# Layer 1's state-space base tables made during layer 0's experts, in the place of the turned tokens, and the second rotation table folded away

## The chip, the cores and the metric

One core of a Trainium2 chip runs the whole kernel in one launch. The metric is device time in microseconds (us), the median of several executions; a profile of one further execution shows where the time goes. The engines are TensorE (PE in the rows, PEld is its weight load), VectorE (DVE), ScalarE (ACT), GpSimd (POOL) and SyncE (SP), which issues most of the DMA transfers. Everything is fp32.

## The reference, cut to what matters

Two layers work on 256 latent and 256 context tokens of width 1024. In each, one projection feeds three mixers, of which the first is a bidirectional diagonal state-space layer (S5); then come an output projection, norms, and a mixture of 64 experts (top 8 a token) with a shared expert.

```python
step = jnp.exp(log_step)[..., None]
a_bar = jnp.exp(lam * step)                      # lam complex, 16 groups x 64 states, 2 directions
b_bar = ((a_bar - 1.0) / lam)[..., None] * b_mat
bu = jnp.einsum('blgc,gpc->blgp', ug, b_bar)
# s_t = a_bar * s_(t-1) + bu_t, forward and backward, context first, then latent
y = einsum(st_f, c_mat[0]).real + einsum(st_b, c_mat[1]).real + ug * d_skip
...
scores = sigmoid(h @ router_w)                   # group-limited top 8, then the experts
out = sum over chosen experts of gate * (silu(h @ w_gate) * (h @ w_up)) @ w_down  + shared
```

The tables that the state-space layer needs depend on parameters alone, not on tokens.

## The kernel before, in words

The program is written as Python generators, woven into one another; a scheduler then orders the instructions on each engine, and waits are semaphores. So an engine executes strictly in an order that is fixed when the program is built, and the text of the code tells that order only roughly.

Layer 0 goes: mixer (0 to about 322 us), `post` (output projection, norms, router; about 322 to 392), experts (about 450 to 1083), combination of the experts' outputs (1083 to 1146). Layer 1 follows with the same stages on the latent tokens alone behind its mixer.

The state-space layer works on chunks of 8 tokens. `s5_prep` (line 474) makes the tables, in this order: exponentials, sine and cosine of 128x16 tiles (`exact_exp`, line 455); `PW`, the powers 0 to 8 of a; `bb`, b_bar; `PA`, powers of a, in the other direction reversed; then `products(q, MT)` for each quarter q of the 16 groups: KT on VectorE (three operations of 128x512 for each of two parts), MT on GpSimd (likewise three), m (TensorE turns MT, ScalarE copies it to M1), kk (KT times bb), kp (kk plus the skip term) and the store of kp to `kd` in DRAM, from where `T` is loaded back. Between the quarters `rotations()` makes `dec`, `Rin` (powers of a's turn per chunk, 64 of them, by doubling), `Rout` (the same times a), and at its end turns half of Rin around by eight copies. Both layers do all of this within their own mixer.

`s5_main` (line 698) then runs four quarters: bu (TensorE) -> rA, rB, Y (VectorE, times Rin) -> scan E with `dec` -> rA, rB, Z (times Rout) -> s5y (TensorE). Projections (`uvs`, `gos`, `rest` in `mixer`, line 1210) run between: pT is a projection with the channels on the partitions (512 or 256 tokens wide), pN one with the tokens on the partitions (256, 80 or 336 columns); `us`, `va`, `krn`, `gpad` and `og` are copies of their results, and gates, zb, e, Bc, AM, qn and kn are of the other two mixers. qr is the first product behind the state-space part.

`moe` (line 1919) has `fT`, the turned tokens of the layer, 128x8x512 floats in a pool tile, read by the router and the shared expert; `spare` is the buffer of the mixers' outputs (`cat2`), free behind the output projection. Into `spare` and a sixth of `sw` the rows x1 are loaded back for the sum in `merging` (line 1849); `ring` holds the experts' weights, loaded by SP in order as buffers come free. Behind layer 0 the experts' outputs Y are loaded into fT for the combination.

Of the kernel before, what the change touches and what calls it, by code (L numbers as in the profile page):

```python
# [190 lines left out]

def zipper(*gens):
# [57 lines left out]
class Trunk:  # L250
    def __init__(self, ctx, tc, d, dbg=None):
# [25 lines left out]
        self.zeros = self.cp.tile([128, 256], F32, name="zeros")  # L277
# [32 lines left out]
    def clear_y(self, l):  # L310
        for i in range(TOK[l] // 128 + 1):
            self.nc.sync.dma_start(self.Y[l][i * 128:(i + 1) * 128].rearrange("p (r f) -> p r f", r=4),
                                   self.zeros[:, None, :].to_broadcast([128, 4, 256]))
# [160 lines left out]
    def s5_prep(self, l, sp, tp):  # L474

        nc, d, v = self.nc, self.d, self.nc.vector
        pv = tp.tile([128, 48], F32, name="pv")
        turn = []
        pm = tp.tile([128, 1024], F32, name="pm")
        dg = tp.tile([128, 4], F32, name="dg")  # L480
        nc.sync.dma_start(pv, d["s5v"][l])
        yield
        nc.sync.dma_start(pm, d["s5m"][l])
        nc.sync.dma_start(dg, d["s5d"][l])
# [8 lines left out]
        self.exact_exp(er, xr, tp, S, "e2")  # L493
# [15 lines left out]
        PW = tp.tile([128, 2, 16, 9], F32, name="PW")  # L509
# [4 lines left out]
        A = tp.tile([128, 2, 16, 32], F32, name="cmA")  # L514
        B = tp.tile([128, 2, 16, 32], F32, name="cmB")
# [8 lines left out]
        for w in (1, 2, 4):  # L524
            cmul(PW[:, 0, :, w + 1:2 * w + 1], PW[:, 1, :, w + 1:2 * w + 1], PW[:, :, :, 1:w + 1],
                 PW[:, 0, :, w], PW[:, 1, :, w], w)

# [16 lines left out]
        bp = tp.tile([128, 2, 16, 32], F32, name="bb")  # L544
        nc.gpsimd.memset(bp[:, :, :, 16:32], 0.0)
        bb = bp[:, :, :, 0:16]
        bx = pm[:, 0:512].rearrange("p (m g c) -> p m g c", m=2, g=16)
        cmul(bb[:, 0], bb[:, 1], bx, wre, wim, 16)
        cx = pm[:, 512:1024].rearrange("p (m g c) -> p m g c", m=2, g=16)

        PA = tp.tile([128, 2, 16, 8], F32, name="PA")
# [31 lines left out]

        dec = sp.tile([128, 16, 65], F32, name="dec")
        R = sp.tile([128, 2, 16, 64], F32, name="Rin")
        Ra = sp.tile([128, 2, 16, 64], F32, name="Rout")
        nc.gpsimd.memset(dec[:, :, 0], 0.0)
        nc.gpsimd.memset(R[:, 0, :, 0], 1.0)
        nc.gpsimd.memset(R[:, 1, :, 0], 0.0)
        nc.gpsimd.memset(Ra[:, :, :, 0], 0.0)  # L590

        def rotations():

            r8, i8, d8, tA, tB = t("r8"), t("i8"), t("d8"), t("tA"), t("tB")
            cr, ci = cs, sn
            for _ in range(3):
                tt(tA, cr, cr, OP.mult)
                tt(tB, ci, ci, OP.mult)
                v.scalar_tensor_tensor(out=i8, in0=cr, scalar=2.0, in1=ci, op0=OP.mult, op1=OP.mult)
                tt(r8, tA, tB, OP.subtract)  # L600
                cr, ci = r8, i8
            tt(d8, er, er, OP.mult)
            tt(d8, d8, d8, OP.mult)
            tt(d8, d8, d8, OP.mult)
            v.tensor_copy(dec[:, :, 1:65], d8[:, :, None].to_broadcast([128, 16, 64]))
            v.tensor_copy(R[:, 0, :, 1], r8)
            v.tensor_copy(R[:, 1, :, 1], i8)
            X, Y = (z[:, 0].rearrange("p g n -> p (g n)").rearrange("p (m g n) -> p m g n", m=2, g=16) for z in (A, B))

            def turn(o, o0, a0, n, yre, yim):  # L610

                x, sh = R[:, :, :, a0:a0 + n], [128, 2, 16, n]
                tt(X[:, :, :, :n], x, yre[:, None, :, None].to_broadcast(sh), OP.mult)
                tt(Y[:, :, :, :n], x, yim[:, None, :, None].to_broadcast(sh), OP.mult)
                tt(o[:, 0, :, o0:o0 + n], X[:, 0, :, :n], Y[:, 1, :, :n], OP.subtract)
                tt(o[:, 1, :, o0:o0 + n], X[:, 1, :, :n], Y[:, 0, :, :n], OP.add)

            for w in (1, 2, 4, 8):
                turn(R, w + 1, 1, w, R[:, 0, :, w], R[:, 1, :, w])
            yield  # L620
            for o, a, n in ((17, 1, 16), (33, 1, 16), (49, 17, 15)):
                w = 16 if o == 17 else 32
                turn(R, o, a, n, R[:, 0, :, w], R[:, 1, :, w])
            yield
            for a, n in ((0, 16), (16, 16)):
                turn(Ra, a + 1, a, n, are, aim)
            yield
            for a, n in ((32, 16), (48, 15)):
                turn(Ra, a + 1, a, n, are, aim)

# [45 lines left out]
        for _ in turns:  # L676
            pass
# [1355 lines left out]
```

## Time and profile before

| | |
|---|---|
| time, 3 runs | 1990.81 us median (1990.21 to 1991.92) |
| profiled execution | 1989.93 us, of which its span 1988.1 |
| granted TensorE clock, mean | 0.956 |
| TensorE busy | 1802.0 us, 91% |
| VectorE, GpSimd, ScalarE busy | 813.2, 456.1, 379.5 us |

The span is what the trace covers; 1.8 us of the execution lie around it. Busy shares are means over stages that have different limits. In the timelines a row is a group of like instructions that follow one another: its start, its length, engine, line, operation, what it writes and reads, and in brackets how long the engine stood before it and what ended that.

### The profile page before, as it was taken

The numbers are of one execution on the slowest core, as the hardware profiler recorded it, in microseconds if no ns is written. First come the engines' busy times: TensorE is split into PE (matmuls) and PEld (weight loads), VectorE is DVE, ScalarE is ACT, GpSimd is POOL, SyncE is SP. The second block draws the span as 40 slices with busy tenths as digits, with TensorE's granted clock in tenths as the row PEclk, the third lists the DMA queues.
The fourth block names the chain that finished last, engine by engine and source line by source line (L and its number), as shares of the span: only waits on it lengthen the run. The fifth ranks groups of instructions, "written<-read, shape, count | busy, mean of one in ns | idle before, by whom it ended". The sixth has DMA issues, their size and how long they took to land. (4 is left out here: it accounts for less than half of the span.)

```text
span 1988.1 us, 29110 instructions
## 1 busy us (share of the span) xinstructions
PE 1802.0 (91%) x10161; PEld 851.0 (43%) x10161; DVE 813.2 (41%) x2298; ACT 379.5 (19%) x739; POOL 456.1 (23%) x453
## 2 busy tenths in 40 slices
PE   6998999879999999899997178899899999999992
PEld 2554665523334333233332055665543354433340
DVE  6856664731223432222121598764731222312113
ACT  2245331201111111001111313341301011110000
POOL 3120211232223232332221551002101211111223
PEclk7999999989999999999999588999999999999996
DMA  8442567399999999999997423256499999899672
GB/s 321 140 96 101 178 250 293 116 319 358 298 326 340 360 323 293 386 377 339 344 297 232 163 75 64 75 213 258 182 372 343 398 353 358 304 385 355 234 261 69
DMA packets 153922, 524.16 MB, mean 264 GB/s; under 512 B 28787, under 2 KB 37939, under 8 KB 145068
## 3 DMA queue, kind: packets, MB, share of 16 engines
q1 hardware_dynamic: 135228, 480.36, 65.1%
q0 software_dynamic: 18544, 41.90, 9.5%
q8 instruction: 82, 1.34, 0.3%
q14 instruction: 68, 0.56, 0.1%
HBM read 531.12 MB, written 47.61 MB: 291 GB/s over the span
## 5 line engine op out<-in xcount | busy, mean ns | idle before, releaser
L1785 PE MATMUL gu<-ring,xT 128*32 128x512 f32 (+5 forms) x2896 | 645.7, 602 | 18.2 <-DMA ring<-in_exp_w 17.7
L1785 PEld LDWEIGHTS gu<-ring,xT 128*32 128x32 f32 (+5 forms) x2896 | 193.7, 129 | 399.3 <-issue 321.2
L1798 PE MATMUL dn<-ring,hT 128*32 128x512 f32 (+5 forms) x1448 | 330.0, 597 | 4.8 <-DMA ring<-in_exp_w 4.0
L1808 POOL DMA_INDIRECT Y<-xo,gi x79 | 119.9, 1518 | 610.8 <-DMA Y<-xo,gi 140.5
L1681 DVE TENSOR_TENSOR hh<-gu,sg 128x256 f32<-128x256 f32 (+4 forms) x86 | 36.5, 424 | 523.2 <-ACT sg L1680 503.7
L1798 PEld LDWEIGHTS dn<-ring,hT 128*32 128x32 f32 (+5 forms) x1448 | 103.1, 128 | 183.2 <-issue 155.7
L1808 POOL DMA_INDIRECT Y<-xo,si x66 | 91.0, 1379 | 302.6 <-DMA Y<-xo,gi 217.4
L1803 DVE TENSOR_SCALAR xo<-dn,gc 128x512 f32<-128x512 f32 (+5 forms) x80 | 60.0, 751 | 229.0 <-PE dn L1798 215.6
L1680 ACT ACTIVATE sg<-gu 128x256 f32<-128x256 f32 (+4 forms) x86 | 32.8, 384 | 586.6 <-PE gu L1785 586.3
L443 PE MATMUL pT<-hT,w 128*128 128x512 f32 (+1 forms) x288 | 120.4, 572 | 4.3 <-DMA w<-in_w_mm 2.7
L1760 PEld LDWEIGHTS <-fb 128*128 128x128 bf16 x1536 | 86.3, 99 | 41.9 <-issue 41.9
L1802 ACT ACTIVATE xo<-dn,gc 128x512 f32<-128x512 f32 (+5 forms) x80 | 55.0, 687 | 253.3 <-PE dn L1798 239.2
L1760 PE MATMUL xT<-oneh,fb 128*128 128x128 bf16 (+4 forms) x1536 | 94.6, 220 | 0.0
L1392 PE MATMUL yo<-w,cat 128*128 128x512 f32 x192 | 83.4, 594 | 0.8 <-DMA w<-in_w_out 0.8
L1762 DVE COPY xT<-xT 128x512 f32<-128x512 f32 (+5 forms) x80 | 53.2, 670 | 70.0 <-PE xT L1760 37.2
L1762 ACT COPY xT<-xT 128x512 f32<-128x512 f32 (+5 forms) x80 | 45.8, 573 | 185.4 <-PE xT L1760 135.3
L443 PEld LDWEIGHTS pT<-hT,w 128*128 128x128 f32 x288 | 56.0, 200 | 58.0 <-issue 47.5
L290 PE MATMUL hT<-cst,xt 128*128 128x128 f32 x64 | 14.6, 404 | 59.3 <-ACT xt L1982 55.2
L451 PE MATMUL pN<-w,hT 128*128 128x256 f32 (+2 forms) x256 | 65.0, 414 | 3.0 <-DVE va L1268 3.0
L342 PE MATMUL ada<-w,sil 128*32 128x512 f32 x384 | 57.9, 649 | 10.4 <-DMA w<-in_ada_w 10.4
L1742 POOL DMA_INDIRECT xg<-fd,gi x48 | 50.3, 1047 | 48.2 <-PE xT L290 19.0
L451 PEld LDWEIGHTS pN<-w,hT 128*128 128x128 f32 x256 | 49.2, 203 | 19.9 <-issue 5.2
(546 smaller groups left out, 2071.1 us busy)
## 6 DMA issues: line engine op xcount, KB each, us to landing
ring<-in_exp_w SPq DMA_DIRECT2D x768, 512.0 KB
w<-in_ada_w SPq DMA_DIRECT2D x48, 1024.0 KB
w<-in_w_out SPq DMA_DIRECT2D x8, 1024.0 KB
sw<-in_sh_w SPq DMA_DIRECT2D x2, 3072.0 KB
w<-in_w_uv SPq DMA_DIRECT2D x4, 1024.0 KB
Y<-zeros SPq DMA_DIRECT2D x8, 512.0 KB
w<-in_w_mm SPq DMA_DIRECT2D x4, 1024.0 KB
w<-in_w_qk SPq DMA_DIRECT2D x4, 768.0 KB
```

The costliest lines, as they stand in the source:

```text
L342: nc.tensor.matmul(ps[32 * q:32 * q + 32, :], self.sil[:, k, :], t[:, q * 512:(q + 1) * 512], start=k == 0, stop=k == 7, tile_position=(0, ...
L443: self.nc.tensor.matmul(ps[base:base + m, n0:NT], w[k][:, col:col + m], hT[:, k, n0:NT], start=k == 0, stop=k == 7)
L451: self.nc.tensor.matmul(ps[:, :n], hT[:, k, i * 128:(i + 1) * 128], w[k][:, col:col + n], start=k == 0, stop=k == 7)
L1392: nc.tensor.matmul(st[at][n], cb[:, i * 128:(i + 1) * 128], wo[n][b], start=b == 0, stop=b == 7)
L1742: nc.gpsimd.indirect_dma_start(out=x[col:col + cap], out_offset=None, in_=self.fd, in_offset=bass.IndirectOffsetOnAxis(ap=si[0:cap], axis= ...
L1760: nc.tensor.matmul(o, self.fb[i][:, z, cs], t["oh"][:, i, 0:m], start=at == 0, stop=at + 1 == len(parts))
L1762: (nc.scalar.copy if hh else v.tensor_copy)(o, a)
L1785: nc.tensor.matmul(t["gu"][r, :], t["xt"][:, 2 * c + b, r], ws[j][:, b * 512:(b + 1) * 512], start=c == 0 and b == 0, stop=c == 3 and b == ...
L1798: nc.tensor.matmul(po[n][r, :], t["ht"][:, b, r], ws[b * nr + j][:, n * 512:(n + 1) * 512], start=b == 0, stop=b == 1, **kw)
L1802: nc.scalar.activation(xo[0:m, 0:512], po[0][0:m], AF.Identity, scale=t["gc"][0:m])
L1803: v.tensor_scalar(out=xo[0:m, 512:1024], in0=po[1][0:m], scalar1=t["gc"][0:m], scalar2=None, op0=OP.mult)
L1808: nc.gpsimd.indirect_dma_start(out=self.Y[l], out_offset=bass.IndirectOffsetOnAxis(ap=si[0:cap], axis=0), in_=xo[col:col + cap], in_offset ...
```

## The change

`s5_prep` is split. `s5_base` makes everything up to PA, the new PB (powers 8 to 1), d8 and the rotation table R, 65 wide with a zero ahead; `s5_tables` makes KT, MT, the copies from R, and T. For layer 1 `s5_base` runs as a generator beside layer 0's route and experts: its temporaries are cut out of `spare` (`Carve`), its results lie in a permanent tile `pz` of 16 KB a partition. `pz` is also what fT now is; so the results may be written only when fT's readers are through. Rout falls away: `Ra` is R shifted by one column, and the factor a that it lacks goes into MT, which takes PB in place of the reversed PA. The eight turning copies and the copy to dec leave VectorE; ScalarE's copies in `finish` take their place. The first x1 row block is still loaded ahead of the experts, two more are now loaded among them, and layer 0's Y are loaded into `spare`. The rest keeps the size of memory (the zeros tile half as wide, the overflow loop, which reloads its tokens).

```diff
+        self.pz = self.cp.tile([128, 4096], F32, name="pz")
...
-    def s5_prep(self, l, sp, tp):
+    def s5_base(self, l, tp):
...
+        z = self.s5_views()
+        R, bp, PA, PB, PW, d8 = (z[n] for n in ("R", "bp", "PA", "PB", "PW", "d8"))
...
+        v.tensor_copy(PB[0:64], PW[0:64, :, :, 8:0:-1])
+        v.tensor_copy(PB[64:128], PW[64:128, :, :, 1:9])
...
+        for w in (1, 2, 4, 8):
+            turn(w + 1, 1, w, w)
+        yield
+        for o, a, n in ((17, 1, 16), (33, 1, 16), (49, 17, 15)):
+            turn(o, a, n, 16 if o == 17 else 32)
+            yield
+
+    def s5_tables(self, l, sp, tp, turns):
...
+        def finish():
+
+            nc.gpsimd.memset(dec[:, :, 0], 0.0)
+            nc.scalar.copy(dec[:, :, 1:65], d8[:, :, None].to_broadcast([128, 16, 64]))
+            for m in range(2):
+                nc.scalar.copy(Rin[0:64, m], R[0:64, m, :, 1:65])
+                for h in range(2):
+                    nc.scalar.copy(Rin[64:128, m, :, 32 * h:32 * h + 32], R[64:128, m, :, 1 + 32 * h:33 + 32 * h][:, :, ::-1])
...
-            for a, n in ((0, 16), (16, 16)):
-                turn(Ra, a + 1, a, n, are, aim)
-            yield
-            for a, n in ((32, 16), (48, 15)):
-                turn(Ra, a + 1, a, n, are, aim)
-
-            for m in range(2):
-                for h in range(2):
-                    z = X[64:128].rearrange("p m g n -> p (m g n)").rearrange("p (g n) -> p g n", g=16)
-                    r = R[64:128, m, :, 32 * h:32 * h + 32]
-                    v.tensor_copy(z, r)
-                    v.tensor_copy(r, z[:, :, ::-1])
...
-            rr, ri = (PA[:, m, g, ::-1][:, :, :, None].to_broadcast(sh) for m in range(2))
+            rr, ri = (PB[:, m, g, :, None].to_broadcast(sh) for m in range(2))
...
-        self.tb = dict(KT=KT, M1=M1, T=T, dec=dec, R=R, Ra=Ra)
+        self.tb = dict(KT=KT, M1=M1, T=T, dec=dec, R=Rin, Ra=R[:, :, :, 0:64])
...
     def merging(self, l, acc, sw, spare, tiles):
...
-        if len(tiles) > 3:
-            nc.sync.dma_start(sw[:, 4], self.x1[l][tiles[3] * 128:(tiles[3] + 1) * 128])
+        for i, t in enumerate(tiles):
+            nc.sync.dma_start(spare[:, i * D:(i + 1) * D] if i < 3 else sw[:, 4], self.x1[l][t * 128:(t + 1) * 128])
...
-            merge = self.merging(l, acc, sw, spare, tiles)
-            for i, t in enumerate(tiles[:3]):
-                nc.sync.dma_start(spare[:, i * D:(i + 1) * D], self.x1[l][t * 128:(t + 1) * 128])
+            early = iter(())
+            if not last:
+                early = self.turns = self.s5_base(l + 1, Carve(spare))
+            merge = chain(early, self.merging(l, acc, sw, spare, tiles))
...
-            beside(work, sh, 1 if last else 2)
+            beside(work, chain(sh, early), 1 if last else 2)
...
-            bufs = [fT[:, 2 * i:2 * i + 2].rearrange("p k n -> p (k n)") for i in range(nt)]
+            bufs = [spare[:, i * D:(i + 1) * D] if i < 3 else sw[:, 4] for i in range(nt)]
```

The order on TensorE at the start of layer 1's mixer, behind the two 512-wide pT, before the change (m_8472 and m_8478 are the two halves of quarter 0, m_8548 and m_8554 of quarter 1; 8 of pN is one token tile):

```order
L451 MATMUL pN<-w,hT 128x256 x32
L451 MATMUL pN<-w,hT 128x80 x8
L290 MATMUL m_8472<-cst,MT 128x128 x4
L290 MATMUL m_8478<-cst,MT 128x128 x4
L571 MATMUL kk<-KT_8361,bb 32x128 x8
L571 MATMUL kk<-KT_8362,bb 32x128 x8
L451 MATMUL pN<-w,hT 128x80 x8
L290 MATMUL m_8548<-cst,MT 128x128 x4
L290 MATMUL m_8554<-cst,MT 128x128 x4
```

And the same place after it (m_8445, m_8451 are quarter 0, m_8518, m_8524 quarter 1):

```order
L474 MATMUL pN<-w,hT 128x256 x16
L313 MATMUL m_8445<-cst,MT 128x128 x4
L313 MATMUL m_8451<-cst,MT 128x128 x4
L649 MATMUL kk<-KT_8373,pz 32x128 x8
L649 MATMUL kk<-KT_8374,pz 32x128 x8
L474 MATMUL pN<-w,hT 128x256 x16
L313 MATMUL m_8518<-cst,MT 128x128 x4
L313 MATMUL m_8524<-cst,MT 128x128 x4
L649 MATMUL kk<-KT_8373,pz 32x128 x8
L649 MATMUL kk<-KT_8374,pz 32x128 x8
L474 MATMUL pN<-w,hT 128x80 x8
```

The first quarter's m and kk have moved between the 256-wide projections, and the 80-wide projection that stood ahead of them has gone behind the second quarter. The other two quarters, an 80-wide pN, bu and the two 336-wide pN with a bu between them follow after the change; before it a 336-wide pN stood ahead of quarter 2 and another behind quarter 3, ahead of the first bu.

The order on VectorE ahead of the first state (rA<-bu) of layer 1, before:

```order
L635 COPY cmA<-Rin 64x512
L636 COPY Rin<-cmA 64x16x32
L578 SCALAR_TENSOR_TENSOR dgt<-cst,dg,kk 128x16
L487 TENSOR_TENSOR kp<-kp,dgt 128x16
L578 SCALAR_TENSOR_TENSOR dgt<-cst,dg,kk 128x16
L487 TENSOR_TENSOR kp<-kp,dgt 128x16
L961 TENSOR_SCALAR zb<-za,cols 128x512
L964 SCALAR_TENSOR_TENSOR zb<-za,cols,zb 128x512 x2
L983 SCALAR_TENSOR_TENSOR e_8959<-G 64x512
L701 TENSOR_TENSOR rA<-bu,Rin 128x512
```

After, from the last operation of KT on:

```order
L690 SCALAR_TENSOR_TENSOR KT_8374<-cmA,cmB 128x512
L1305 COPY va<-pN 128x4x64
L656 SCALAR_TENSOR_TENSOR dgt<-cst,dg,kk 128x16
L629 TENSOR_TENSOR kp<-kp,dgt 128x16
L1305 COPY va<-pN 128x4x64 x2
L656 SCALAR_TENSOR_TENSOR dgt<-cst,dg,kk 128x16
L629 TENSOR_TENSOR kp<-kp,dgt 128x16
L1315 COPY gpad<-pN 128x4x4 x2
L656 SCALAR_TENSOR_TENSOR dgt<-cst,dg,kk 128x16
L629 TENSOR_TENSOR kp<-kp,dgt 128x16
```

Two more rows, dgt and kp again, then `gpad<-pN 128x4x4 x2` (the two 336-wide pN) stand behind these, and then rA. Rotations and turning copies are gone, zb and e are behind rA, and all four gpad copies are ahead of it.

The order on VectorE in the fourth state, from its scan E to its Z, after the change:

```order
L761 SCALAR_TENSOR_TENSOR E<-dec,Y 128x260 x2
L1007 TENSOR_TENSOR AM<-G,Bc 64x512
L735 TENSOR_TENSOR rA<-E,pz 128x512
L735 TENSOR_TENSOR rB<-E,pz 128x512
L1028 SCALAR_TENSOR_TENSOR AM<-zero,AM 32x512
L1030 SCALAR_TENSOR_TENSOR AM<-zero,AM 32x256
L1007 TENSOR_TENSOR de<-AM,cst 32x32
L1031 SCALAR_TENSOR_TENSOR AM<-zero,AM 32x256
L1007 TENSOR_TENSOR e_8968<-Bc,AM 64x512
L1007 TENSOR_TENSOR de<-AM,cst 32x32
L1042 TENSOR_SCALAR e_8968<-e_8968 64x512
L735 TENSOR_TENSOR Z<-rA,rB 64x256
```

Before, at that place:

```order
L727 SCALAR_TENSOR_TENSOR E<-dec,Y 128x260 x2
L961 TENSOR_SCALAR zb<-za,cols 128x256
L701 TENSOR_TENSOR rA<-E,Rout 128x512
L701 TENSOR_TENSOR rB<-E,Rout 128x512
L964 SCALAR_TENSOR_TENSOR zb<-za,cols,zb 128x256
L701 TENSOR_TENSOR Z<-rA,rB 64x256
```

Seven operations of the gates (AM, de, e), of which some stood in the earlier states and some behind the last Z, now stand between rB and Z of the last state; zb of the last block has gone behind Z.

## Rows read from the trace of the kernel before

**Rows 1.** Windows: length, busy us (instructions) of PE, PEld, DVE, ACT, POOL; PEclk, DMA, GB/s

```profile
1146.00:1290.00 144.00, 118.77 (x655) 81.76 (x655) 122.16 (x296) 39.09 (x75) 34.52 (x43) 0.89 0.27 74
1290.00:1432.00 142.00, 134.09 (x745) 77.16 (x744) 84.55 (x253) 48.76 (x99) 18.33 (x26) 0.99 0.54 204
1432.00:1950.00 518.00, 513.20 (x3618) 220.08 (x3616) 124.65 (x415) 56.03 (x102) 92.18 (x65) 1.00 0.90 332
```

**Rows 2.** Timeline of TensorE in layer 1's mixer

```profile
1146.43 15.29 PE L443 MATMUL pT<-hT,w 128*128 128x512 f32 x32
1161.56 15.72 PE L451 MATMUL pN<-w,hT 128*128 128x256 f32 x80
...
1181.78 2.35 PE L451 MATMUL pN<-w,hT 128*128 128x80 f32 x16 [3.03 <-DVE va L1268]
1190.73 1.09 PE L290 MATMUL m<-cst,MT 128*128 128x128 f32 x4 [6.60 <-DVE va L1268]
...
1196.55 6.66 PE L451 MATMUL pN<-w,hT 128*128 128x336 f32 x16
...
1216.92 1.89 PE L712 MATMUL bu<-U,M 128*128 128x64 f32 x16
...
1258.52 0.69 PE L746 MATMUL s5y<-KT,Z 128*64 128x128 f32 x2 [5.16 <-DVE Z L701]
...
1270.61 0.45 PE L746 MATMUL s5y<-KT,Z 128*64 128x128 f32 x4 [0.22 <-DVE Z L701]
...
1286.56 0.70 PE L845 MATMUL qr<-qn,w 128*128 128x256 f32 x2 [1.47 <-DVE qn L797]
```

**Rows 3.** Timeline of VectorE in layer 1's mixer

```profile
1148.65 0.17 DVE L460 TENSOR_SCALAR e1xc<-pv 128x16 f32<-128x16 f32 x1
...
1210.23 0.69 DVE L487 TENSOR_TENSOR cmA<-Rin,PW 128x512 f32<-128x512 f32 x1
...
1218.63 0.42 DVE L635 COPY cmA<-Rin 64x512 f32<-64x512 f32 x1
...
1229.46 0.69 DVE L701 TENSOR_TENSOR rA<-bu,Rin 128x512 f32<-128x512 f32 x1
...
1268.83 1.73 DVE L701 TENSOR_TENSOR Z<-rA,rB 64x256 f32<-64x256 f32 x4
```

**Rows 4.** Groups by form, VectorE, 1162 to 1183: busy, mean ns, idle before

```profile
L487 DVE TENSOR_TENSOR cmB<-PA,pm 128x512 f32<-128x512 f32 x4 | 6.4, 1591 | 0.0
L487 DVE TENSOR_TENSOR cmA<-PA,pm 128x512 f32<-128x512 f32 x4 | 4.4, 1104 | 0.0
```

**Rows 5.** The same groups of VectorE from 1206 to 1210, GpSimd idle

```profile
L487 DVE TENSOR_TENSOR cmB<-PA,pm 128x512 f32<-128x512 f32 x2 | 1.4, 684 | 0.0
```

**Rows 6.** Timeline of GpSimd in layer 1's mixer

```profile
1161.40 1.05 POOL L659 TENSOR_TENSOR cmA<-PA,bb 128x512 f32<-128x512 f32 x1 [13.94 <-DVE PA L553]
...
1187.60 1.05 POOL L659 TENSOR_TENSOR cmA<-PA,bb 128x512 f32<-128x512 f32 x1
...
1195.85 1.38 POOL L659 TENSOR_TENSOR MT<-cmA,cmB 128x512 f32<-128x512 f32 x1 [6.14 <-PE m L290]
```

**Rows 7.** Timeline of ScalarE, the end of the combination

```profile
1143.39 1.23 ACT L1982 ACTIVATE xt<-acc,nb,a3rs 128x1024 f32<-128x1024 f32 x1
```

**Rows 8.** Timeline of SP, DMA issues in layer 1's mixer

```profile
1173.84 2.08 SPq L329 DMA_DIRECT2D w<-in_w_mm  x2
1201.65 6.28 SPq L582 DMA_DIRECT2D kd<-kp  x8
```

**Rows 9.** Windows, shorter ones of layer 1's mixer

```profile
1176.00:1180.00 4.00, 2.75 (x52) 2.31 (x51) 3.97 (x5) 1.71 (x5) 3.84 (x4) 1.00 1.00 399
...
1190.00:1205.00 15.00, 11.66 (x100) 7.85 (x101) 14.79 (x28) 3.11 (x8) 5.54 (x4) 0.65 0.02 6
```

**Rows 10.** Timeline of VectorE in layer 0, `post` and experts

```profile
349.41 0.69 DVE L1401 TENSOR_TENSOR pt<-yo,g 128x512 f32<-128x512 f32 x1 [1.93 <-PE yo L1392]
...
495.38 0.42 DVE L1681 TENSOR_TENSOR hh<-gu,sg 128x256 f32<-128x256 f32 x1 [15.56 <-ACT sg L1680]
```

More of the change, by code (lines that the diff above doesn't have):

```diff
@@ L189, in beside, with chain, __init__, tile @@
             next(side, None)
+def chain(*gens):
+    for g in gens:
+        yield from g
+class Carve:
+    def __init__(self, at):
+        self.at, self.n, self.got = at, 0, {}
+    def tile(self, shape, dt, name):
+        if name not in self.got:
+            n = math.prod(shape[1:])
+            self.got[name] = self.at[:, self.n:self.n + n]
+            self.n += n
+            assert self.n <= self.at.shape[1]
+        a = self.got[name]
+        if len(shape) == 4:
+            a = a.rearrange("p (a b c) -> p a b c", a=shape[1], b=shape[2])
+        return a if dt == F32 else a.bitcast(dt)
 def zipper(*gens):
@@ L552, in s5_prep @@
         v.tensor_copy(PA[0:64], PW[0:64, :, :, 0:8])
         v.tensor_copy(PA[64:128], PW[64:128, :, :, 7::-1])
-        yield
+        v.tensor_copy(PB[0:64], PW[0:64, :, :, 8:0:-1])
+        v.tensor_copy(PB[64:128], PW[64:128, :, :, 1:9])
+        r8, i8, tA, tB = t("r8"), t("i8"), t("tA"), t("tB")
+        cr, ci = cs, sn
+        for _ in range(3):
+            tt(tA, cr, cr, OP.mult)
+            tt(tB, ci, ci, OP.mult)
+            v.scalar_tensor_tensor(out=i8, in0=cr, scalar=2.0, in1=ci, op0=OP.mult, op1=OP.mult)
+            tt(r8, tA, tB, OP.subtract)
+            cr, ci = r8, i8
@@ new lines, in s5_base @@
+        for w in (1, 2, 4, 8):
+            turn(w + 1, 1, w, w)
+        yield
+        for o, a, n in ((17, 1, 16), (33, 1, 16), (49, 17, 15)):
+            turn(o, a, n, 16 if o == 17 else 32)
+            yield
+    def s5_tables(self, l, sp, tp, turns):
+        nc, d, v = self.nc, self.d, self.nc.vector
+        z = self.s5_views()
+        R, bp, PA, PB, d8 = (z[n] for n in ("R", "bp", "PA", "PB", "d8"))
+        bb = bp[:, :, :, 0:16]
+        pm = tp.tile([128, 512], F32, name="pmc")
+        dg = tp.tile([128, 4], F32, name="dg")
+        nc.sync.dma_start(pm, d["s5m"][l][:, 512:1024])
+        nc.sync.dma_start(dg, d["s5d"][l])
+        cx = pm.rearrange("p (m g c) -> p m g c", m=2, g=16)
+        tt = lambda o, a, b, op: v.tensor_tensor(out=o, in0=a, in1=b, op=op)
+        A, B = (tp.tile([128, 2, 16, 32], F32, name=n) for n in ("cmA", "cmB")) if l else self.cm
+        turn = []
@@ L640, in s5_prep @@
+        Rin = sp.tile([128, 2, 16, 64], F32, name="Rin")
         for _ in range(pace("turn0", l, 0)):
@@ L677, in s5_prep @@
             pass
+        finish()
         yield
@@ L1224, in mixer @@
         tp = P(ps_, "s5tmp", side="right")
-        prep = self.s5_prep(l, sp, tp)
+        if l == 0:
+            base = self.s5_base(0, tp)
         if l == 0:
@@ L1230, in mixer @@
             next(ada)
-            next(prep)
+            next(base)
             xt = [self.ln_load(l, i) for i in range(4)]
@@ L1238, in mixer @@
             weave(ada)
-            next(prep)
+            for _ in range(4):
+                next(base)
             load("uv")
@@ L1249, in mixer @@
             self.zp = P(zs, "z")
+            self.turns = base
         zp = self.zp
@@ L1309, in states @@
         def states():
-            yield from prep
+            yield from self.s5_tables(l, sp, tp, self.turns)
             ps_.close()
@@ L1923, in moe @@
         units = plan(l)
-        acc = mq.tile([128, nt, D], F32, name="acc")
+        acc = self.pz[:, 2048:].rearrange("p (i n) -> p i n", i=nt) if last else mq.tile([128, nt, D], F32, name="acc")
         with ExitStack() as es:
```

102 lines of the change are left out of this document (44 added, 58 removed).

## The prediction

> **What bounds the kernel now.** I read the profile in the order from stage to instruction. The windows [rows 1] first: the expert stages keep TensorE busy throughout, but between 1146 and 1290, in layer 1's mixer, it works 118.8 of 144 us while VectorE works 122.2. So there VectorE, not TensorE, is the full engine, and this is the stage that the change touches most. The timeline of TensorE [rows 2] tells which wait ends last. After two projections (pT, pN) it stands until VectorE has copied `va` (3.03 and 6.60 us), and its last large wait (5.16) and a small one behind it (0.22) are for Z, the last product of VectorE's state chain. The timeline of VectorE [rows 3] shows why everything is late. From 1148.65 it makes the base of the tables (exponentials, powers, `bb`), and GpSimd, which makes MT, has nothing to do until 1161.40: it waited 13.94 us for PA [rows 6]. Then VectorE works through KT, the rotations (Rin, Rout), the turning copies, and only at 1229.46 begins the first state (rA), though its `bu` was ready at 1218.8 [rows 2]. Idle time of TensorE is 25.2 us in this stage [rows 1], and that is nearly all that there is to win here. To it comes the low clock: granted 0.65 from 1190 to 1205 [rows 9], behind the wait of 6.60. A 336-wide pN takes 6.66 us there, and by its columns it would take 4.8 at the pace of the pN from 1161.56 on (15.72 us for 1104 columns) [rows 2].
>
> **The change part by part.**
>
> *What leaves layer 1's mixer.* The base, 1148.65 to 1161.40, 12.8 us of VectorE. The rotation table R, made among the KT pieces: I take its three wide turns and the four short ones at about the size of Rout's four, which ran from 1210.23 to 1218.63, 8.4 us [rows 3]. Rout itself, 8.4 us. The eight turning copies, 0.42 each, 3.4 us. Some 33 us of VectorE go; TensorE's order cannot give all of it back, so I walk through the new order with the old durations.
>
> *GpSimd.* Its first MT product waits only for the temporaries' place, which the last xt of the combine holds until 1143.39 + 1.23 = 1144.6 [rows 7]. Six pieces took 1161.40 to 1187.60, 4.4 us each; alone I take 3.4 (the cmA of 1187.60, which ran alone, took 1.05, and MT costs a fifth more) [rows 6]. MT has two buffers: the wait of 6.14 at 1195.85 was for TensorE's m of the quarter two before [rows 6]. That wait stays, and shapes what follows: the third quarter's first MT must wait for m of the first.
>
> *VectorE.* KT starts where the base started, 1148.65. Beside GpSimd its operations took 1.10 and 1.59 us, alone 0.68 [rows 4, 5]; I take 1.30, for 24 of them 31.2, with three copies of 0.4 between: KT ends at 1181. The va copy that frees the bank of the second m stands behind the last KT.
>
> *TensorE.* Anchor: pT begins at 1146.43 as before, since the combine ahead of it is the same chain. Two pT end at 1161.56. The 15.72 us of the next row are 4 x 256 + 80 columns, so a 256-wide pN costs 3.65 and an 80-wide 1.1. Two pN: 1168.9. m and kk of a quarter fill 1177.1 to 1178.75 (where the idle 3.03 begins), 1.6: 1170.5. Two pN: 1177.8. m of quarter 1 waits for va at 1181: with kk 1182.3. pN80 1183.4, m and kk of quarter 2 1185. GpSimd's seventh MT was held until m of quarter 1 (1181.7), ends 1183.1, its eighth piece alone 3.4 later, 1186.5: m and kk of quarter 3 end at 1187.8. pN80 1188.9, bu 1190.8 (1216.92 + 1.89 before), pN336 1195.6, bu 1197.4, pN336 1202.2 (at 4.8, since TensorE has now stood little). VectorE has the `gpad` copies of both wide pN in its queue ahead of rA, so rA begins about 1202.5, not when bu is ready at 1190.8. Before it was 1229.46: 27 us earlier.
>
> *The state chain.* It ran from 1229.46 to 1270.56, 41.1 us [rows 3]. In the order after it holds the same four states, the same gate work between them, and now also the AM scans and the zb of the first block; those that went ahead before (zb, e) and those that came after (the end of AM, about 2 us) make no big difference: 41 again, Z ends 1243.6. TensorE will have done its pT by 1232 and stands some 12 us.
>
> *Behind Z.* From 1270.56 to qr at 1286.56 it took 16.0 us [rows 2]. In the new order two 256-wide pT more stand there (half of a 512-wide one, 15.29/4 = 3.8 at most, say 3.6 each), while the gap of 1.47 before qr may close: 22.2. So qr comes at 1265.8, 20.8 us earlier. From there the order of TensorE is the old one and the rest moves along. One deduction: a stand of 12 us is longer than the 6.60 behind which the clock was 0.65; for the first pT after it I take 1.5 us (6.66 against 4.8 is 1.9) [rows 2, 9]. Layer 1: -19.3.
>
> *What is paid in layer 0.* The same base work, 12.8 + 8.4 or some 21 us of VectorE, and two table loads of ScalarE, now lie in the post stage and among the experts. Its long tail (bb, the doubling of R) falls behind the last shared gate product, where VectorE stood 15.56 us [rows 10]; hidden, and if it were not, hh of an expert would be late by up to 8.4. Its head stands in the gap of 1.93 us in which VectorE waited for yo [rows 10], but its first operation waits for a load of `pv` into cat2, which may go out only when TensorE has read that part of cat2 for yo. If the load lands 2 us after, the norm of the third token tile is late by 2 to 4 us; four gaps behind it can take it up. Bounds 0 and 4, I take 1. Two 512 KB loads of x1 move from before the experts into their last third: at 399 GB/s [rows 9] 2.6 us if nothing hides them, 0 if the ring is ahead; I take 0.5. ScalarE's new copies (dec, Rin) and layer 0's own base: modc behind one more product of 0.68, 0.6. In layer 0's mixer Rout and the copies go too, 12 us of VectorE. I count nothing for it: TensorE there works through its projections, and the end of the state chain is fed by bu products whose place in its order stays. Sum +2.
>
> *Sum.* -19.3 + 2 = -17.3. The profiled execution took 1989.93 us, 1.8 more than its span, and the median is 1990.81; from the median this gives 1973.5.
>
> **A rule that speaks against it.** KT and MT ran side by side, and both slowed: 1.59 for 0.68, 4.4 for about 3.4 [rows 4 to 6]. In the new order they run together from the first operation. The Trainium skill ("SBUF — State Buffer", section "SBUF: two separate sides") says that VectorE with two SBUF inputs and GpSimd exclude each other for a whole instruction. By that rule each KT operation beside GpSimd would cost its own 0.68 and one of GpSimd's, 1.05 to 1.3, about 1.8. The trace agrees in part only: 1.3 is the mean, and in 4.4 us of GpSimd's piece fit more than three of VectorE's operations.
>
> **The rivals.**
> 1. *The bigger gain.* VectorE has 20 us less to do, so KT may see less of GpSimd (0.68 instead of 1.30 for the last third saves 5 us), rA comes at 1197 and the clock does not fall: 25 to 29 us at most, the whole idle time of the stage and the slow pN. 1962 to 1968.
> 2. *SP's queue.* The w_mm loads were issued at 1173.84 [rows 8]; in the new order they stand behind the eight kd stores of quarters 0 and 1. kp of these waits behind KT until 1182, eight issues took 6.3 us [rows 8] and follow after quarter 1: w_mm goes out at 1189 and is in by 1199 (before, both were done within 10 us, the DMA engines full at 399 GB/s [rows 9]). pT needs it at 1204. With 5 us of slack it is hidden; if a store waits for the one before it to land, pT is 4 to 8 us late, and T, which is issued behind w_qk, too: 1978 to 1983.
> 3. *Full exclusion of KT and MT.* 24 operations, of which half meet GpSimd at 1.8 and the rest run in its waits: KT ends 3.5 us later, and all behind it: 1977.
> 4. *The gain is given back.* After qr a load or the route waits anyway. Against it: TensorE is busy 134.1 of 142 us behind 1290 [rows 1], so nothing there waits for a long load now; only if the loads of ada_w set that pace does the time stay within 0.2%.
> 5. *Slower.* Base operations stand in VectorE's queue ahead of the route in layer 0. If pv comes late (4) and each of the operations delays the route, whose chain starts the expert loads, the whole base is paid there: 12.8 + 8.4 + 4 is 25.2, against 19.3 won: 1996.7. It decides from 19.3 us of exposure on. For it speaks that VectorE executes in order and the norm chain of four token tiles runs there, against it that the order puts the operations into its gaps and only the head before the expert loads.
>
> **How the numbers follow.** A difference under 0.2% (4 us) is about what a measurement of this kernel can't tell from no change. The forecast as worked out, 1969 to 1978: 0.48. Rival 1: 0.16. Rival 2: 0.13. Rival 3: 0.05. Rival 4: 0.07 as no change, and 0.03 where only part is given back (1984 to 1987). Rival 5: 0.08. Faster 0.85, same 0.07, slower 0.08. The range 1962 to 1984 takes in the forecast and rivals 1 to 3 and leaves out the last two.
>
> **What would show it.** GpSimd's first MT near 1145 and KT from 1149 in the profile of the changed kernel; the first rA between 1199 and 1206; a wait of TensorE for Z of about 10 us near 1232, and qr 20 us earlier in relation to the first pT. The step is wrong if TensorE waits for DMA of w_mm or T there, if KT ends behind 1185, or if the state chain is longer than 43 us. Layer 0 is wrong if the first pT of layer 1 is not within 3 us of 1148.4, which is 1146.4 and the 2 us paid.

## The result, and the profile after

The changed kernel took 1970.29 us (median of 4 runs, 1966.15 to 1972.08) beside 1991.37 us for the kernel before in the same job: a ratio of 0.9891 with a 95% interval of 0.9874 to 0.9909, 21 us. Run again in the last job it took 1964.90 us (5 runs, 1961.47 to 1969.73), ratio 0.9864 (0.9845 to 0.9882). The forecast was 1973.5, the range 1962 to 1984. The profiled execution took 1969.44 us, 1.9 more than its span.

The stage windows of the changed kernel answer to [rows 1] (same columns, the stages cut at the same places in the program):

```profile
1147.00:1273.00 126.00, 115.06 (x655) 81.18 (x654) 83.64 (x140) 46.85 (x81) 32.18 (x40) 0.93 0.32 81
1273.00:1415.00 142.00, 135.20 (x748) 78.70 (x748) 85.69 (x268) 47.22 (x99) 18.33 (x26) 0.97 0.56 206
1415.00:1930.00 515.00, 511.07 (x3598) 217.98 (x3598) 122.79 (x409) 55.34 (x101) 91.90 (x65) 1.00 0.90 333
```

Layer 1's mixer is 18 us shorter. VectorE lost 38.5 us of work there (122.16 to 83.64), TensorE has the same 655 products, and its idle time fell from 25.2 to 10.9 us. The two stages behind it keep their lengths within 3 us. TensorE's timeline in that mixer answers to [rows 2]:

```profile
1147.58 15.61 PE L466 MATMUL pT<-hT,w 128*128 128x512 f32 x32
...
1180.94 0.63 PE L313 MATMUL m<-cst,MT 128*128 128x128 f32 x4 [1.83 <-DVE dgt L656]
...
1182.45 3.70 PE L474 MATMUL pN<-w,hT 128*128 128x80 f32 x16
...
1193.94 4.74 PE L474 MATMUL pN<-w,hT 128*128 128x336 f32 x16
...
1244.74 0.69 PE L780 MATMUL s5y<-KT,Z 128*64 128x128 f32 x2 [6.83 <-DVE Z L735]
...
1269.69 1.13 PE L879 MATMUL qr<-qn,w 128*128 128x256 f32 x4
```

From the first pT to qr it is 122.1 us, before 140.1. The waits in the products, five before with 16.2 us in all (3.03, 6.60 and 2.50 for va, 2.59 and 1.51 for KT), are one of 1.83; the wait for Z has grown from 5.16 to 6.83 and is now the largest. VectorE and GpSimd answer to [rows 3] and [rows 6]:

```profile
1149.44 1.52 DVE L629 TENSOR_TENSOR cmA<-pz,pmc 128x512 f32<-128x512 f32 x1
...
1166.24 0.69 DVE L690 SCALAR_TENSOR_TENSOR KT<-cmA,cmB 128x512 f32<-128x512 f32 x1
...
1205.27 0.17 DVE L1315 COPY gpad<-pN 128x16 f32<-128x16 f32 x1 [6.13 <-ACT krn L1314]
1205.73 0.69 DVE L735 TENSOR_TENSOR rA<-bu,Rin 128x512 f32<-128x512 f32 x1 [0.29 <-DVE gpad L1315]
...
1214.45 0.54 DVE L995 TENSOR_SCALAR zb<-za,cols 128x512 f32<-128x512 f32 x1
...
1243.84 1.73 DVE L735 TENSOR_TENSOR Z<-rA,rB 64x256 f32<-64x256 f32 x4
```

```profile
1145.84 1.06 POOL L692 TENSOR_TENSOR cmA<-pz 128x512 f32<-128x512 f32 x1 [1.63 <-ACT xt L2030]
...
1171.12 1.27 POOL L692 TENSOR_TENSOR MT<-cmA,cmB 128x512 f32<-128x512 f32 x1 [5.46 <-PE m L313]
```

GpSimd starts MT before the first pT instead of 15 us behind it; VectorE starts KT where the base used to start, and begins the first state (rA) 58.2 us behind the first pT, before 83.0.

### The profile page after: what moved, and what is told of

It is laid out like the page before. It is cut to its first block, busy times and chain, and to the rows that moved or that the text cites. A ratio compares the mean times of both kernels' runs of the same rounds, so it can differ in the third digit from the quotient of the medians.

```text
span 1967.5 us, 29068 instructions
## 1 busy us (share of the span) xinstructions
PE 1801.8 (92%) x10161; PEld 851.9 (43%) x10161; DVE 779.2 (40%) x2252; ACT 394.2 (20%) x756; POOL 453.7 (23%) x453
## 5 line engine op out<-in xcount | busy, mean ns | idle before, releaser
L1429 PEld LDWEIGHTS yo<-w,cat 128*128 128x128 f32 x192 | 36.2, 190 | 45.7 <-issue 43.8
```

Of the source, the lines that this page charges most:

```text
L1429: nc.tensor.matmul(st[at][n], cb[:, i * 128:(i + 1) * 128], wo[n][b], start=b == 0, stop=b == 7)
```

## The experiments

Each is the changed kernel with the edit shown or told; gpad_lag1, gpad_lag3_zb, double_base and after_again share a job. The stretch is the time from layer 1's first pT to qr in the profile; "Z" is TensorE's wait for the last Z. Each stretch comes from one profile, and its first two pT alone take 14.5 to 16.1 us, so small differences in it mean little.

```
kernel           median us (runs)   ratio to before [95%]      first pT   stretch   Z
changed          1970.29 (4)        0.9891 [0.9874, 0.9909]    1147.58    122.11    6.83
after_again      1964.90 (5)        0.9864 [0.9845, 0.9882]    1144.48    121.64    6.82
base_in_place    1992.09 (10)       1.0006 [0.9995, 1.0017]    1143.68    148.71    1.22
unfolded         1977.84 (4)        0.9934 [0.9910, 0.9959]    1144.56    127.79    6.82
gpad_act         1968.28 (4)        0.9902 [0.9873, 0.9932]    1144.83    119.08    6.83
gates_late       1981.25 (5)        0.9953 [0.9935, 0.9971]    1148.75    130.48    none
gpad_mca         1975.93 (4)        0.9935 [0.9916, 0.9953]    1149.10    121.66    none
gpad_zbact       1969.87 (4)        0.9904 [0.9888, 0.9921]    1147.34    117.47    4.69
base0_late       1966.63 (4)        0.9888 [0.9870, 0.9906]    1148.03    119.17    6.82
no_mt            1957.76 (1)        one run                    1144.47    116.48    6.82
gpad_lag1        1959.27 (5)        0.9840 [0.9821, 0.9859]    1146.62    112.26    none
gpad_lag3_zb     1964.69 (5)        0.9875 [0.9857, 0.9893]    1143.83    119.30    none
double_base      1967.11 (5)        0.9883 [0.9863, 0.9903]    1146.30    118.87    6.82
```

**base_in_place** takes the early base away and keeps the rest.

```diff
+            if l:
+                self.turns = self.s5_base(l, tp)
+                for _ in range(5):
+                    next(self.turns)
+                yield
             yield from self.s5_tables(l, sp, tp, self.turns)
...
-                early = self.turns = self.s5_base(l + 1, Carve(spare))
```

> Layer 1's base tables are made in layer 1's own mixer again, ahead of its products; the folded rotation table, the copies on ScalarE and everything of layer 0's mixer stay as in the changed kernel. Theory A (the early base is the gain, since the products wait for it): GpSimd's first MT product stands some 13 to 15 us behind layer 1's first pT, TensorE's waits for the products come back (16.3 us of them in the kernel before), the stretch from the first pT to qr is 133 to 136 us (140.1 before, 122.1 with the change), the total 1981 to 1985 us. Theory B (the fold is the gain, since the second table and its turning lay between Rout and rA, 19 us of VectorE): 122 to 127 us and 1970 to 1975 us. Layer 0's own mixer should be as early as in the changed kernel (slots load at about 393 us), and its experts should lose nothing any more: if the early base costs them, the last dn comes up to 3 us sooner.

The whole gain is gone, more than theory A expected. VectorE and then TensorE:

```profile
1202.24 0.69 DVE L688 SCALAR_TENSOR_TENSOR KT<-cmA,cmB 128x512 f32<-128x512 f32 x1
...
1223.91 0.55 DVE L993 TENSOR_SCALAR zb<-za,cols 128x512 f32<-128x512 f32 x1 [7.79 <-ACT za L989]
...
1226.85 0.69 DVE L733 TENSOR_TENSOR rA<-bu,Rin 128x512 f32<-128x512 f32 x1
```

```profile
1187.65 1.08 PE L313 MATMUL m<-cst,MT 128*128 128x128 f32 x4 [8.21 <-DVE va L1303]
...
1234.36 0.66 PE L778 MATMUL s5y<-KT,Z 128*64 128x128 f32 x2 [9.07 <-issue]
```

The waits in the products are back (8.21 the largest, 16.5 us in all), and the fold does not help rA: VectorE has no table left to make between 1207 and 1227, but the first convolution (zb) stands ahead of rA in its queue and waits for za, which TensorE makes late. rA is 83.2 us behind the first pT, as before. So the fold without the early base brings rA nothing here; the order of VectorE's queue takes it. But the run takes away more than the early base: its stretch is 8.6 us longer than that of the kernel before, since in its new order TensorE also stands 9.07 us ahead of the first s5y (the profile names no releaser; VectorE makes the first Z from 1233.31 on) and 5.71 us for gT. It shows that the gain needs the early base in this order, not what the fold alone would be worth in a better one.

**unfolded** keeps the early base and multiplies the second table out again, in layer 1 alone.

```diff
+                for a, n in ((1, 16), (17, 16), (33, 16), (49, 15)):
+                    x, sh = R[:, :, :, a:a + n], [128, 2, 16, n]
+                    tt(X[:, :, :, :n], x, are.to_broadcast(sh), OP.mult)
...
-            rr, ri = (PB[:, m, g, :, None].to_broadcast(sh) for m in range(2))
+            rr, ri = ((PA[:, m, g, ::-1][:, :, :, None] if l else PB[:, m, g, :, None]).to_broadcast(sh) for m in range(2))
```

> The base stays early; in layer 1 alone the second rotation table is multiplied out again (16 VectorE operations, in place) and the products take the powers that they took before. Theory A: VectorE idles some 19 us between the last KT and rA, the 16 operations fit in there, the stretch from first pT to qr stays at 122 to 124 us, the total within 2 us of the changed kernel's 1970. Theory B: rA comes 8 to 9 us later and with it the end of layer 1's mixer: 130 us, total 1978.

The total is theory B's, the stretch between the two: 5.7 us more than the changed kernel's. VectorE's idle time was there, but the 16 operations were not in it. They stand from 1177.26 on, ahead of the last va copies:

```profile
1177.26 0.69 DVE L629 TENSOR_TENSOR cmA<-pz 128x512 f32<-128x512 f32 x1
...
1188.24 0.42 DVE L1314 COPY va<-pN 128x256 f32<-128x256 f32 x1
```

and TensorE waits 3.35 and 3.02 us for va copies behind them (and 0.97 for one ahead of them), the last of these here:

```profile
1188.80 1.08 PE L313 MATMUL m<-cst,MT 128*128 128x128 f32 x4 [3.02 <-DVE va L1314]
```

So of the 18.0 us in the stretch 12.3 come from the early base (with the copies on ScalarE, which no run takes apart from it) and 5.7 from the fold on top of it. The 5.7 is the low end: the changed kernel's profile holds a fall of the clock (below), and against the profiles of the same layer 1 without it, 118.9 and 119.2, the fold is worth 8.6 to 8.9 (in unfolded the clock fell too, behind its own waits: granted 0.50 from 1181 to 1193).

**gpad_act** takes away what rA waited for, with TensorE's order unchanged.

```diff
-                nc.vector.tensor_copy(self.gpad[:, i, :, 0:4], ps[:, 64:80].rearrange("p (q h) -> p q h", q=4))
+                (nc.scalar.copy if l else nc.vector.tensor_copy)(self.gpad[:, i, :, 0:4], ps[:, 64:80].rearrange("p (q h) -> p q h", q=4))
```

> In layer 1 the four copies of the gate columns (gpad) go from VectorE to ScalarE; the order on TensorE is the same. Theory A (rA and the last dgt stand on VectorE behind the gpad copies of both wide pN): rA at 47 to 51 us behind the first pT instead of 58, TensorE's wait of 6.83 us for the last Z falls below 1 us, qr 6 to 7 us sooner, total 1963 to 1965 us. Theory B (rA is held by the landing of the kd stores, whose memory it takes, or by bu): rA moves by less than 3 us, total 1968 to 1972.

Both theories fell, though rA came where A said. VectorE's timeline:

```profile
1193.25 0.69 DVE L735 TENSOR_TENSOR rA<-bu,Rin 128x512 f32<-128x512 f32 x1 [5.51 <-DMA kd<-kp]
...
1201.44 0.68 DVE L735 TENSOR_TENSOR rB<-bu,Rin 128x512 f32<-128x512 f32 x1
1208.26 0.55 DVE L995 TENSOR_SCALAR zb<-za,cols 128x512 f32<-128x512 f32 x1 [6.14 <-ACT za L991]
...
1237.65 1.73 DVE L735 TENSOR_TENSOR Z<-rA,rB 64x256 f32<-64x256 f32 x4
```

rA came 9.7 us sooner (48.4 us behind the first pT; what it waits for now is the landing of kd), and nothing followed: in the second quarter zb stands between rB and Y and now waits 6.14 us for za. From zb to the end of the last Z it is 31.1 us here as in the changed kernel (1214.45 to 1245.57). ScalarE copies za once TensorE has made its pT, wherever rA starts, and so TensorE meets the same 6.83 us. The stretch of 119.1 is no gain: base0_late and double_base, whose layer 1 is the changed kernel's, have 119.2 and 118.9 (the 122.1 is a matter of the clock, below).

**gates_late** and **gpad_mca** move the scans of the gates behind the last Z by an entry of the pace table: for layer 1 `'rest': ('G', 'CM', 'A')`, and with gpad on ScalarE `'rest': ('G', 'MCA')`.

> In layer 1 the gates' scans come behind the convolutions and the inputs of the attention in the program instead of between them. Theory A (8.8 us of the gates' VectorE operations stand inside the state chain, ahead of the last Z): the chain from rA to the last Z falls from 39.8 to some 31 us, TensorE's 6.83 us for Z vanish, qr is 5 to 7 us sooner and the total 1963 to 1966 us. Theory B (the scans are then late for the mLSTM, which takes the wait over, or the convolutions take their place ahead of Z): no gain or up to 3 us lost.

> The gpad copies on ScalarE as in gpad_act, and in layer 1 the inputs of the attention come ahead of the convolutions and those ahead of the gates, so that in VectorE's queue no convolution stands inside the first three quarters of the state chain and the gates' scans stand behind the last Z. Theory A (in gpad_act the chain stood 6.14 us for za behind rB of the second quarter, and the scans of 8.8 us stood ahead of the last Z): TensorE no longer waits for Z, the stretch from first pT to qr falls from gpad_act's 119.1 to 111 to 114 us. Theory B (the scans, now late, make amT wait, or the convolutions come late for their own readers, as when the gates were put last): 118 us or more.

In both the wait for Z vanishes, and in both theory B names what follows, though in gpad_mca with another wait than it named. TensorE in gates_late, then in gpad_mca:

```profile
1276.01 0.69 PE L313 MATMUL amT<-cst,AM 128*128 128x128 f32 x2 [11.64 <-DVE AM L1030]
```

```profile
1217.07 3.63 PE L466 MATMUL pT<-hT,w 128*128 128x512 f32 x4 [7.21 <-DMA w<-in_w_qk]
```

With the gates last, amT waits 11.64 us for their scans ahead of qr and glu 4.83 us for gT. The stretch is 11.3 to 11.6 us longer than the 118.9 to 119.2 of the profiles in which, as here, the clock stayed up in the products; theory B had said up to 3. With the attention's inputs first, their weights (w_qk, issued at 1201.51 and 1207.38) are asked for too late.

**gpad_zbact** also sends the convolution's first product to ScalarE (`nc.scalar.activation` with scale and bias for `tensor_scalar`, in layer 1).

> As gpad_act, and the first product of layer 1's convolutions (zb from za) goes from VectorE to ScalarE; TensorE's order is the same. Theory A (VectorE's queue stands for za in the middle of the second quarter of the state chain): Y of that quarter starts 6 us sooner, the next operation that needs za stands behind E, so that about 3.5 us are won in all, TensorE's wait for the last Z falls from 6.83 to some 3.3 us, the stretch to 115 to 116 us. Theory B (the wait for Z is set by something else): it stays at 6.8 us and the stretch at 119.

```profile
1212.23 0.75 DVE L1001 SCALAR_TENSOR_TENSOR zb<-za,cols,zb 128x512 f32<-128x512 f32 x1 [3.95 <-ACT zb L996]
```

Theory A in direction: the wait for za moves behind E and shrinks from 6.14 to 3.95, the one for Z from 6.83 to 4.69. That is 2.1 us where 3.5 were expected, and it shows in the stretch (from the third bu to qr 63.0 us, in gpad_act 65.2), not in the total.

**gpad_lag1** and **gpad_lag3_zb** set the pace of layer 1 to `'lag': 1` and `'lag': 3` with `'rest': ('G', 'CMA')`, the first on gpad_act, the second on gpad_zbact.

> As gpad_act, and in layer 1 the readout follows the states by one quarter instead of two, with the gates behind the inputs of the attention; in VectorE's queue the first two quarters of the state chain now stand ahead of anything that needs za, and most scans behind the last Z. Theory A (the 6.83 us for Z stand because the chain waits for za behind rB of the second quarter, and 8.8 us of scans lie ahead of the last Z): TensorE's wait for Z falls below 3 us, the stretch from first pT to qr to 112 to 115 us (119.0 to 119.2 where the clock doesn't fall), total 1962 to 1966. Theory B (kn, now ahead of the last quarter, waits for the root that ScalarE makes, and the wait only moves): stretch 118 to 121, total as the changed kernel.

> As gpad_zbact (gpad and the first product of the convolutions on ScalarE), with the readout three quarters behind the states in layer 1 and the gates last: no scan stands ahead of the last Z. Theory A: the chain from rA to the last Z falls from 39.8 to 34 to 36 us (the 4 us for za remain in the second quarter), TensorE's wait for Z is gone, the stretch is 112 to 115 us, total 1962 to 1966. Theory B (the scans, now late, make amT wait, or TensorE's waits move to za and ss): 118 us or more, total as the changed kernel or slower.

VectorE in gpad_lag1:

```profile
1195.50 0.69 DVE L735 TENSOR_TENSOR rA<-bu,Rin 128x512 f32<-128x512 f32 x1 [5.43 <-DMA kd<-kp]
...
1210.95 0.55 DVE L995 TENSOR_SCALAR zb<-za,cols 128x512 f32<-128x512 f32 x1 [0.38 <-ACT za L991]
...
1226.53 0.75 DVE L831 SCALAR_TENSOR_TENSOR kn<-pT,cols,zb 128x512 f32<-128x512 f32 x1 [5.85 <-ACT zb L829]
```

Two quarters are done before zb, which then waits 0.38 us. kn does wait 5.85 for ScalarE, as theory B said, but TensorE has its own work meanwhile: its longest wait is 1.20 us, the stretch 112.3. That is 9.4 us off the 121.6 of the changed kernel in the same job, of which some 3 are the clock's fall there, and the total is 5.6 us lower than the changed kernel's in the same job (0.9840 against 0.9864; the intervals overlap a little). It is the fastest full version that was run. In gpad_lag3_zb theory B holds. ScalarE, then TensorE:

```profile
1242.39 0.63 ACT L1004 ACTIVATE mqk<-zb 128x512 f32<-128x512 f32 x1 [6.91 <-DVE zb L1001]
1242.92 0.35 ACT L782 COPY s5y<-s5y 128x256 f32<-128x256 f32 x1
```

```profile
1243.33 1.97 PE L313 MATMUL yT<-cst,s5y 128*128 128x128 f32 x8 [7.46 <-ACT s5y L782]
```

The copy of the last readout stands in ScalarE's queue behind an activation that waits for VectorE's zb, which is behind the scans: the wait has only changed its name.

**no_mt** leaves out layer 1's MT products on GpSimd (`nc.gpsimd.memset(MT, 0.0)` in their place).

> Leaves out layer 1's MT products on GpSimd (the tile is only set to zero), so the states of layer 1 are not those of the reference. Theory A (VectorE's KT products take 1.3 to 1.6 us each because GpSimd works beside them): they take 0.69 us throughout, the last KT ends some 17 to 18 us behind the first pT instead of 33, TensorE's first waits in the products vanish (1.8 us). Theory B (it is their own shape or place of memory): they stay at 1.4 us and more.

Theory A: all 24 KT operations take 0.68 or 0.69 us, and the last ends 20.1 us behind the first pT instead of 32.9:

```profile
1163.93 0.69 DVE L690 SCALAR_TENSOR_TENSOR KT<-cmA,cmB 128x512 f32<-128x512 f32 x1
```

All of this contention is worth 2.4 to 2.7 us of the stretch (116.5 against 118.9 to 119.2 where the clock stayed up). Against the changed kernel's own profile it is 5.6, since without MT TensorE does not wait in the products at all and the clock does not fall there either.

**base0_late** puts layer 0's base back behind the turned input; **double_base** makes layer 1's base twice beside the experts.

```diff
-            for _ in range(4):
-                next(base)
             load("uv")
...
+            if l == 0:
+                for _ in range(4):
+                    next(self.turns)
```

```diff
-                early = self.turns = self.s5_base(l + 1, Carve(spare))
+                at = Carve(spare)
+                early = self.turns = chain(self.s5_base(l + 1, at), self.s5_base(l + 1, at))
```

> In layer 0 the base's later parts come again behind the turned input, right ahead of the products, as in the kernel before; layer 1 as in the changed kernel. Theory A (the 4 us that layer 0's mixer won come from the order on VectorE: the second half of us before the products, so U and w_mm are asked for sooner): TensorE waits 2 to 3 us for w_mm again, ss is at 132 to 133 us, lg at 350 us. Theory B (they come from the other edits): ss stays at 128.7 to 130 us, lg at 346 to 347. In both the first expert's weights may give part of it back; the total is up to 4 us more than the changed kernel's by A, the same by B.

> Layer 1's base is made twice, one behind the other, beside layer 0's experts (93 VectorE operations and two loads more); the rest as in the changed kernel. Theory A (the early base lies in VectorE's idle time beside the experts and costs nothing): total within 2 us of the changed kernel, last dn of layer 0 not later. Theory B (it costs, 2 us in the prediction and 7 to 8 by the rival that ends slower): the second one costs the same again, 2 to 8 us, to be seen between the slots and the last dn of layer 0.

> The changed kernel itself once more, to be compared with the other three on the same chip and to see whether its stretch from first pT to qr is 122.1 us again (clock fallen to 0.63 for 6 us where TensorE had waited 1.83 us for dgt) or 119.2 as in base0_late, whose layer 1 is the same and where that wait was 0.62 us and the clock stayed up. Theory A (the fall of the clock is worth 3 us and comes by chance of the waits ahead of it): 119 or 122, total 1966 to 1972. Theory B: always 122.

In base0_late the wait for w_mm does not return; ss is at 131.75 and lg at 348.80, between the two theories, and the total is that of the changed kernel. A second base costs nothing that can be told: 1967.11 against 1964.90 us, intervals overlapping, last dn at 1082.2 against 1081.5. The second base lies among the experts alone (782 to 821 us), so the run says nothing of the head of the first one, which stands in the post stage. after_again had 121.6, which both of its theories allow; but the wait alone does not decide on the clock, since double_base waited the same 1.83 us as the changed kernel and its clock stayed up.

## Why the prediction was right, point by point

**The products (right).** GpSimd's first MT was forecast at 1144.6 and stood at 1145.84, 1.7 us ahead of the first pT as worked out; KT was to run from 1148.65 to 1181 and ran from 1149.44 to 1180.5. The mean of 1.30 came near (1.26 measured) by a mixture that was not foreseen: 1.42 to 1.65 where GpSimd worked (one of 1.20), 0.69 from 1166.24 to 1170.96, while GpSimd waited 5.46 us for m. That this wait would stay was said. VectorE lost 38.5 us of work in this stage where some 33 were listed: the turns of R, taken at 8.4, had been 17.7 us in the kernel before, some of them beside GpSimd. The sum for layer 1 does not use that figure.

**rA (right in time, wrong in weight).** Forecast 56 us behind the first pT, measured 58.2, and it was the gpad copies that held it. But gpad_act shows that nothing hangs on it. The step that failed is "the state chain, 41 again" counted from rA: the chain measures 39.8 us in the changed kernel and 46.1 with the earlier rA, because its fixed piece is the 31.1 us from the first zb, and za ties that to TensorE's own pT. The end of Z came out right (98.0 us behind the first pT, forecast 97.2) by luck: in this order za, which the prediction did not look at, is done at 1214.32, when VectorE comes to zb at 1214.45. With an earlier rA the same reasoning would have failed, as it did in gpad_act's theory A.

**TensorE's stand for Z (mis-sized: 12 forecast, 7.0 measured).** TensorE was to be through by 85.6 us behind the first pT and was at 90.3: some 3 us are the fall of the clock in the products, 1.1 a wait of ss for za. The tail from the last Z to qr was 24.1, forecast 22.2 and 1.5 for the clock (the prediction's own terms, 16.0 and twice 3.6 less the gap of 1.47, give 21.7).

**The clock (foreseen behind Z, not in the products, and not certain there).** The 1.5 us were charged for a fall behind the wait for Z. It came: the first pT behind that wait took 4.45 us, the next one 3.62.

```profile
1248.44 4.45 PE L466 MATMUL pT<-hT,w 128*128 128x256 f32 x16
...
1253.59 3.62 PE L466 MATMUL pT<-hT,w 128*128 128x256 f32 x16
```

A second fall came earlier, in the products, and was in no term of the sum. Two windows of the changed kernel, then the same pieces of double_base, which waited the same 1.83 us for dgt:

```profile
1178.00:1184.00 6.00, 4.17 (x51) 3.28 (x50) 4.68 (x9) 1.59 (x4) 4.12 (x4) 0.81 0.21 25
1184.00:1190.00 6.00, 6.00 (x81) 5.25 (x88) 0.33 (x2) 2.00 (x5) 2.41 (x3) 0.63 0.51 169
```

```profile
1176.50:1182.50 6.00, 4.17 (x60) 3.47 (x59) 4.20 (x9) 1.59 (x4) 4.12 (x4) 1.00 0.15 35
1182.50:1188.50 6.00, 5.62 (x102) 4.65 (x101) 0.18 (x1) 2.63 (x6) 2.47 (x3) 1.00 0.55 187
```

With the second fall the stretch is 121.6 to 122.1, without it 118.9 to 119.2. The forecast of 120.9 lies between.

**Layer 0 (the price about as forecast, the gain missed).** "I count nothing" for layer 0's mixer was wrong: U is issued at 58.45 instead of 64.37 us and w_mm at 65.38 instead of 68.92, and TensorE's wait for w_mm is gone. The row of the kernel before, then of the changed one:

```profile
75.31 3.70 PE L443 MATMUL pT<-hT,w 128*128 128x512 f32 x8 [2.56 <-DMA w<-in_w_mm]
```

```profile
71.43 7.03 PE L466 MATMUL pT<-hT,w 128*128 128x512 f32 x16
```

lg came 4.1 us sooner (350.49 to 346.35). Which of the edits brings that is shown in part only: with the base's later parts put back (base0_late) w_mm is issued at 66.71, the wait stays away, and lg has 1.7 of its 4.1 us left. Most of the lead is given back behind lg: the last ten dn of layer 0 start at 1080.97 against 1081.64. A part of that is the price that was forecast. From lg to the first slot, where the head of the early base stands on VectorE, the twelve profiles with an early base take 46.65 to 48.04 us (median 47.35), the two without it (before and base_in_place) 45.95 and 45.92: 0.7 to 2.1 us, where the prediction took 1. From the slots to the last dn the two and the twelve overlap (686.6 and 687.1 us; 686.2 to 690.8), and double_base bears out that base operations among the experts cost nothing that can be told. TensorE's gate products there wait 17.6 us, nearly all for the expert weights, and 16.6 before, so the loads are the likely taker of the rest, which is argued, not shown. Over the ten profiles with this layer 0 the first pT of layer 1 lies between 1143.8 and 1149.1, 1146.2 in the mean, where the one profile of before has 1146.43: about 0 in all for the +2 of the sum.

**The sum (right, in part by luck).** Layer 1: -18.0 measured for -19.3; without the second fall of the clock, which the sum did not hold, it would be about -21. Layer 0: +1.15 in this profile for +2, a price near the forecast and a gain that was left out. The span is 20.6 us shorter, 17.7 of it by the first slot of layer 1 (1431.0 to 1413.3); the other 2.9 lie behind that. From there to the end the two profiles of the changed kernel took 554.2 and 558.2 us, all profiles with the same code there 551.5 to 559.1, so no cause is given for it.

**The rivals.** The bigger gain (1): the second measurement, 1964.90, lies in its range, but not by its mechanism, since rA stands at 1205.73, not 1197, and the clock fell. SP's queue (2) did not bind here, with no wait for w_mm or T, but gpad_mca shows how near it is: one change of order, and w_qk costs 7.21 us. The full exclusion of KT and MT (3) fell: KT ended at 1180.5, not 3.5 us late. That 3.5 does not follow from the rival's own terms either, since 12 operations at 1.8 and 12 at 0.68 make 29.8 us, less than the 31.2 of the forecast. Where both engines work without a wait, three operations of each take 4.6 us; alone they take 2.1 (no_mt) and 3.4, and one after the other would be 5.5. The Trainium skill ("SBUF — State Buffer", section "SBUF: two separate sides") would have the one block the other for a whole instruction; the measured 4.6 is nearer to that than to no contention, but not equal to it. And the whole contention is worth 2.4 to 2.7 us beside an equal clock, so neither reading could have moved the forecast far. The gain given back behind qr (4): not so, the first slot of layer 1 is 17.7 us sooner and the end 20.6. Rival 5, the whole base paid in layer 0, is refuted by two readings: its head costs 0.7 to 2.1 us between lg and the slots, and double_base shows that the part among the experts costs nothing that can be told.

## What to carry to other kernels

Work taken off an engine that executes in order is worth what stands behind it in the queue, not its length: the same 16 operations cost 5.7 to 8.9 us because they stood ahead of three small copies, and 9.7 us of earlier start were worth nothing because one later operation waited for another engine. Before costing a chain from its first operation, look in its middle for one that waits for the very engine that waits for the chain. And when a wait vanishes, read the next run for its new name (za, AM, w_qk, s5y) before counting it as won.

## What was not expected of the hardware

The same wait ahead of the same work gave both levels of TensorE's clock: behind 1.83 us for dgt the granted clock was 0.63 over some 6 us in the changed kernel and stayed at 1.00 in double_base, where TensorE was busy for the same 4.17 of the 6 us around the wait; gpad_lag1 waited 2.24 us there and kept 1.00. Three of twelve profiles with this order of products show the fall (pN of 80 columns: 3.70 us instead of 2.01): both of the changed kernel, and unfolded, whose waits there are longer. What decides it stays open.
